# Opening stages of a hybrid encoder layer: loads in a fixed order, the first token blocks beside the memory's products, and stores on GpSimd's queue

## The chip, the core and the metric

One core of one Trainium2 chip runs the whole kernel. The metric is the device time of one execution in microseconds (us), given as the median of three runs. The profile shows one more execution of the same program. Its engines are TensorE (PE, with its weight loads PEld), VectorE (DVE), ScalarE (ACT), GpSimd (POOL) and SyncE (SP). SP computes nothing here: it issues transfers. GpSimd computes and issues transfers too.

## The reference

The kernel computes one encoder layer with three branches that read one combined projection:

```python
h = rms_norm(x, norm_pre_w)                       # x: 2048 tokens x 1024
proj = h @ w_in                                   # 1024 x 5648 columns
aq, ak, av, bqkv, ba, bb, mq, z = split(proj)
y_a = axial_gqa_attention(rope(rms_norm(aq)), rope(rms_norm(ak)), av)     # 8 heads, 2 of k and v
y_b = rms_norm(bidir_gated_deltanet(silu(conv(bqkv)), ba, bb))            # 4 heads, both directions
mkv = rms_norm(mem, mem_norm_w) @ w_mem_kv        # 256 memory tokens: 512 columns of keys, 512 of values
y_m = memory_cross_attention(mq, mk, mv)          # 4 heads
mix = concat(y_a, y_b, y_m) * silu(z)
out = x + rms_norm(mix @ w_out, norm_post_w)
```

The change touches only the opening: the memory keys and values, the norm of x, and the projection to `av`, `ba` and `bb`.

## The kernel before

Products are made in pairs of a high and a low part: each operand is split in two (`hi` is a cast, `lo` the remainder), and three products (hi hi, hi lo, lo hi) are added in PSUM. ScalarE makes the casts, VectorE most remainders.

**Who sets the order.** The program is traced in the order of its text, and a planner then orders each engine's instructions by simulated times, so an instruction can be issued earlier than its place in the text. A transfer made with `dma` (line 63, on SP) or `wdma` (line 74, on GpSimd) may be moved so. `late_dma` (line 68) issues on SP and is pinned: it can't go ahead of the instruction that was traced on SP just before it. Every engine works through its own list in order, and a transfer that waits for its data or its buffer holds those behind it.

**The memory (lines 305 to 378).** Two blocks of 128 memory tokens are loaded, normed, turned by TensorE (`turned`, PSUM tiles `tp_m`) and split (`mT`). `w_mem_kv` comes in four groups of 256 columns, each in two halves of 512 KB. `mem_load` (line 323) loads a half into `mraw` (two buffers) and splits it into `whi` and `wlo`; `mem_group` (line 341) makes 48 matmuls and brings the result out (`mkt` for keys, `mvt` for values). The loop at line 366 loads group g + 1 ahead of product g. In it also stand the load of the value weights (`load_group` at g = 2, the 272 columns of `av`, `ba`, `bb`; tiles `wraw` and `wparts`) and of the norm's weights (`wpre`, `wcol`).

**The tokens (lines 380 to 453).** There are 16 blocks of 128 tokens, in five rounds over q. `tok_norm(q)` (line 392) loads four blocks (tile `x`, nine buffers shared with the two memory blocks; `late_dma`), takes their squares on ScalarE, and their roots and scaling on VectorE. `tok_turn(q, kc)` (line 407) turns four pieces of 128 x 128 in one PSUM tile (tag `tp`, four buffers) and splits them into `hT` with the norm's weights. `av_proj(tb)` (line 414) makes 24 matmuls into a PSUM tile (tag `mm`, four buffers), brings the result out as `ab` and `vt` (two buffers), takes a maximum and stores `vt` to DRAM. Rounds q = 0 to 3 turn blocks 4q to 4q + 3, rounds 1 to 4 project those of the round before. Round 1 also scales and stores the memory's keys and values (`mem_keys`, `mem_values`; tiles `mk16` and `mv16` in the tag `wn`, one buffer that `wmem` and `wpre` have used before). Rounds 1 and 2 load and scale the key and query norm weights (`qk_weights`, three small transfers each). Round 3 loads the weights of the first query and key group (`wraw` through GpSimd; GpSimd also does one multiply and one subtraction for them).

Behind this stage come the key and query projections, the DeltaNet branch, attention and the output product. They aren't changed.

Of the kernel before, what the change touches and what calls it, by code (L numbers as in the profile page):

```python
# [11 lines left out]
F32 = mybir.dt.float32  # L12
# [11 lines left out]
D = 1024  # L24
# [4 lines left out]
KC = D // 128  # L29
# [8 lines left out]
def hybrid_layer(ctx: ExitStack, tc: tile.TileContext, t: dict, out, dbg=None):  # L38
# [24 lines left out]
    def dma(to, of):  # L63
        if to.dtype == F32R:
            to, of = to.bitcast(F32), of.bitcast(F32)
        Q.dma_start(to, of)

    def late_dma(to, of):

        Q.pinned = True  # L70
        dma(to, of)
        Q.pinned = False

    def wdma(to, of):
        if to.dtype == F32R:
            to, of = to.bitcast(F32), of.bitcast(F32)
        nc.gpsimd.dma_start(to, of)  # L77
# [3 lines left out]
    const2 = p0.enter_context(tc.tile_pool(name="const2", bufs=1, side="right"))  # L81
# [7 lines left out]
    v_d = scratch("v", [TB, 128, 256])  # L89
    v16_d = scratch("v16", [128, 2, TB, 256], F16)  # L90
    mqT_d = scratch("mqT", [4, 128, 2, S], F16)
    mkT_d = scratch("mkT", [128, 2, 4, NMEM], F16)
    mv16_d = scratch("mv16", [128, 2, 2, 512], F16)
# [30 lines left out]
    vs, mvs, hs_, mks, qns, kns = (scales[:, i:i + 1] for i in range(6))  # L124
# [118 lines left out]
    def norm_scale(w, s, cs, n=0, least=2.0 ** -90, to=None):  # L243

        m = const2.tile([128, 1], F32, tag="nsm", name="nsm", bufs=2)
        e = const2.tile([128, 1], I32, tag="nse", name="nse", bufs=2)
        V.tensor_reduce(m, w, axis=AX.X, op=ALU.max, apply_absolute_value=True)
        V.tensor_scalar(m, m, least, None, op0=ALU.max)
        V.tensor_scalar(e, m.bitcast(I32), 0x7f800000, None, op0=ALU.bitwise_and)
        V.tensor_scalar(s.bitcast(I32), e, -1.0, float((263 + n) << 23), op0=ALU.mult, op1=ALU.add)  # L250
        V.tensor_scalar(cs.bitcast(I32), e, 1.0, -float((9 + n) << 23), op0=ALU.mult, op1=ALU.add)
        to = w if to is None else to
        V.tensor_scalar(to, to, s, None, op0=ALU.mult)
# [23 lines left out]
    def load_group(*args, **kw):  # L277
        _, loaded = begin_group(*args, **kw)
        return loaded
# [12 lines left out]
    with tc.tile_pool(name="s0", bufs=1) as p:  # L292
# [13 lines left out]
        wpre = p.tile([128, D], F32, tag="wn", name="wpre")  # L306
# [16 lines left out]
        def mem_load(g):  # L323
            wg = []
            for half in range(2):
                raw = p.tile([128, 4, 256], F32, tag="mraw", name="mraw", bufs=2)
                dma(raw, t["w_mem_kv"][0, 512 * half:512 * half + 512, g * 256:g * 256 + 256].rearrange("(k p) c -> p k c", p=128))
                pool, tag = (p, "mhl") if g % 2 else (wp, "whl")
                hi, lo = (pool.tile([128, 4, 256], F32R, tag=tag, name=n, bufs=4) for n in ("whi", "wlo"))
                A.copy(hi, raw)  # L330
                V.tensor_tensor(lo, raw, hi.bitcast(F32), op=ALU.subtract)
                wg.append((hi, lo))
            return wg

        wg = mem_load(0)
# [5 lines left out]
        def mem_group(g, wg):  # L341
            ps = mm_ps(f"mem{g}", (128, 2, 256))
            for u in range(2):
                sl = slice(u * 128, u * 128 + 128)
                n = 0
                for kc in range(KC):
                    hi, lo = wg[kc // 4]
                    k = kc % 4
                    for i, (m_, w_) in enumerate(((0, hi), (1, hi), (0, lo))):
                        st, sp = (n == 0), (n == 3 * KC - 1)  # L350
                        if g < 2:
                            T.matmul(ps[:, u, :], w_[:, k, sl], mT[m_][:, kc, :], start=st, stop=sp)
                        else:
                            T.matmul(ps[:, u, :], mT[m_][:, kc, sl], w_[:, k, :], start=st, stop=sp)
                        n += 1
            if g >= 2:
                mv = mvt[:, :, (g - 2) * 256:(g - 1) * 256]
                A.copy(mv, ps)
                V.tensor_reduce(mvmax[:, g - 2:g - 1], mv, axis=AX.XY, op=ALU.max, apply_absolute_value=True)
                return  # L360
            mk = mkt[:, 2 * g:2 * g + 2]
            A.copy(mk, ps)
            V.tensor_reduce(mkmax[:, g:g + 1], mk, axis=AX.XY, op=ALU.max, apply_absolute_value=True)

        mkt = p.tile([128, 4, NMEM], F32, tag="mkt", name="mkt")
        for g in range(4):
            nxt = mem_load(g + 1) if g < 3 else None
            if g == 2:
                wav, (avcs,) = load_group([(1280, 256), (3072, 16)], dma)
            if g == 1:  # L370
                late_dma(wpre, t["norm_pre_w"].to_broadcast([128, D]))
                wcol = const2.tile([128, KC], F32, name="wcol")
                late_dma(wcol, t["norm_pre_w"].rearrange("o (k p) -> p (o k)", p=128))
                norm_scale(wpre, hs_, hcs, to=wcol)
            mem_group(g, wg)
            wg = nxt
        hT.extend(hpool.tile([128, 2, KC, 512], F16, tag="B16", name=f"hT{b}", bufs=6, align_bytes=512).rearrange("p i k c -> i p k c") for b in range(4))
        hs = {}

        def qk_weights(which):  # L380

            nw = t["k_norm_w"] if which == 0 else t["q_norm_w"]
            wb = const2.tile([128, 2, 128], F32, name=f"wb{which}")
            dma(wb[:, 0, :], nw.to_broadcast([128, 128]))
            nv = nw.rearrange("o (a s d) -> o a s d", a=2, s=2)
            wv = wb[:, 1, :].rearrange("p (a s d) -> p a s d", a=2, s=2)
            for s_ in range(2):
                dma(wv[:, :, s_, :], nv[:, :, 1 - s_, :].to_broadcast([128, 2, 32]))
            norm_scale(wb.rearrange("p a d -> p (a d)"), *((kns, kncs) if which == 0 else (qns, qncs)), n=1, least=2.0 ** -45)
            return wb  # L390

        def tok_norm(q):

            ss = p.tile([128, 4], F32, tag="ss", name=f"ss{q}", bufs=2)
            rst = p.tile([128, 4], F32, tag="rst", name=f"rst{q}", bufs=2)
            hs[q] = []
            for j in range(4):
                tb = 4 * q + j
                xt = p.tile([128, D], F32, tag="x", name=f"x{tb}", bufs=9)
                late_dma(xt, t["x"][0, tb * 128:(tb + 1) * 128, :])  # L400
                row_stats(xt, ss[:, j:j + 1], hT[q][0][:, 2 * j:2 * j + 2, :])
                hs[q].append(xt)
            rsqrt(p, rst, ss, [128, 4], 1.0 / D, EPS)
            for j in range(4):
                V.tensor_scalar(hs[q][j], hs[q][j], rst[:, j:j + 1], None, op0=ALU.mult)
# [8 lines left out]
        def av_proj(tb):  # L414
            ps = mm_ps(f"av{tb}")
            tok_proj(ps[:, 0:272], wav, tb)
            A.activation(ab[:, tb, :], ps[:, 256:272], AF.Copy, scale=avcs)
            vt = p.tile([128, 256], F32, tag="vt", name=f"vt{tb}", bufs=2)
            A.activation(vt, ps[:, 0:256], AF.Copy, scale=avcs)
            V.tensor_reduce(vmax[:, tb:tb + 1], vt, axis=AX.X, op=ALU.max, apply_absolute_value=True)  # L420
            dma(v_d[tb], vt)

        def mem_values():
            pow2_scale(mvmax, mvs, mvcs, "mv")
            mv16 = p.tile([128, 2, 2, 512], F16, tag="wn", name="mv16")
            A.activation(mv16[:, 0], mvt, AF.Copy, scale=mvs)
            V.scalar_tensor_tensor(mv16[:, 1], mvt, mvs, mv16[:, 0], op0=ALU.mult, op1=ALU.subtract)
            dma(mv16_d, mv16)

        def mem_keys():  # L430
            pow2_scale(mkmax, mks, mkcs, "mk")
            mk16 = p.tile([128, 2, 4, NMEM], F16, tag="wn", name="mk16")
            split_evac(mkt, mk16[:, 0], mk16[:, 1], mks)
            dma(mkT_d, mk16)

        wbs = []
        tok_norm(0)
        for q in range(5):
            if q in (1, 2):
                wbs.append(qk_weights(q - 1))  # L440
# [3 lines left out]
            if q == 3:  # L444
                nxt = load_group([(1024, 256)])
# [11 lines left out]
    with tc.tile_pool(name="s1", bufs=1) as p:  # L457
# [49 lines left out]
        for which in range(2):  # L507
            wb = wbs[which]
# [19 lines left out]
            for g in range(1 if which == 0 else 4):  # L528
                wg, (qcs,) = nxt
                for b in range(4):  # L530
                    if g == 0 and b < 3:
                        tables(b + 1)
                    if b == 1:
                        nxt = load_group([((which + g) * 256 if which + g < 4 else 1536, 256)])
# [49 lines left out]
    with tc.tile_pool(name="s2", bufs=1) as p:  # L584
        wg, bcs, xbs, svs, kts_ = {0: nxt[0]}, {0: nxt[1]}, {}, {}, {}
# [248 lines left out]
    with tc.tile_pool(name="s3g", bufs=1, side="right") as p:  # L834
# [4 lines left out]
        xa, ax, u, s_, s2, acc = (tmp(n) for n in ("xa", "ax", "u", "s_", "s2", "acc"))  # L839
# [69 lines left out]
    with tc.tile_pool(name="s3a", bufs=1) as sv0:  # L909
        p = rows  # L910
# [24 lines left out]
        for hp in range(2):  # L935
            p = (sv0, sv1)[hp]
# [3 lines left out]
            for d in range(2):  # L940
                for b in range(4):
                    o = 64 * d + 16 * b
# [13 lines left out]
            for d, ft in enumerate(((rr, ni), (ni, rr))):  # L956
                for n in range(2):
                    for b in range(4):
                        o = 64 * d + 16 * b
# [648 lines left out]
```

## Time and profile before

| what | value |
|---|---|
| runs | median 2408.82 us (2407.42 to 2410.19, three runs) |
| profiled execution, its own time | 2418.02 us |
| its span | 2416.0 us |
| TensorE busy | 2316.7 us (96%) |
| VectorE, ScalarE, GpSimd busy | 1637.6, 1298.9, 703.2 us |
| first product of the memory | 18.79 us |
| last value product ends, first key and query product starts | 116.06 us |

A row of the order of time gives the start and the length in us, the engine, the line, the operation, what it writes and reads by the program's names, its shape and count, and in brackets how long the engine had been idle before it and what ended that. Nearly all rows name line 51, through which every engine's instructions are issued, so tile names tell them apart: `m`, `tp_m`, `mT` and `mem` are the memory's, `x`, `tp` and `hT` the tokens', `av` and `vt` the value product's. In a row by stretches each engine's busy time stands in front of its count of instructions.

### The profile page before, as it was taken

The numbers are of one execution on the slowest core, as the hardware profiler recorded it, in microseconds if no ns is written. First come the engines' busy times: TensorE is split into PE (matmuls) and PEld (weight loads), VectorE is DVE, ScalarE is ACT, GpSimd is POOL, SyncE is SP. The second block draws the span as 40 slices with busy tenths as digits, with TensorE's granted clock in tenths as the row PEclk, the third lists the DMA queues.
The fourth block names the chain that finished last, engine by engine and source line by source line (L and its number), as shares of the span: only waits on it lengthen the run. The fifth ranks groups of instructions, "written<-read, shape, count | busy, mean of one in ns | idle before, by whom it ended". The sixth has DMA issues, their size and how long they took to land. (4 is left out here: it accounts for less than half of the span.)

```text
span 2416.0 us, 42155 instructions
## 1 busy us (share of the span) xinstructions
PE 2316.7 (96%) x15838; PEld 1466.6 (61%) x15846; DVE 1637.6 (68%) x3304; ACT 1298.9 (54%) x2508; POOL 703.2 (29%) x432
## 2 busy tenths in 40 slices
PE   6999999999999899999999999999999999899998
PEld 6888864455554347667664566666666666544443
DVE  6687658999758745555553778777888877355553
ACT  5634436544443145555543888888888788111110
POOL 0155431112211221121020554444444445122120
PEclk9999999999999999999999999999999999999999
DMA  6457656334487466677865999999999999775551
GB/s 232 144 137 162 123 118 188 101 111 126 146 254 214 106 201 212 205 221 219 249 201 192 232 248 242 246 240 244 239 250 241 246 240 231 202 248 187 178 183 53
DMA packets 949500, 471.58 MB, mean 195 GB/s; under 512 B 723184, under 2 KB 898864, under 8 KB 949040
## 3 DMA queue, kind: packets, MB, share of 16 engines
q1 hardware_dynamic: 936848, 425.89, 69.6%
q0 software_dynamic: 12448, 43.00, 5.3%
q8 instruction: 125, 2.05, 0.3%
q14 instruction: 79, 0.65, 0.1%
HBM read 207.60 MB, written 108.10 MB: 131 GB/s over the span
## 5 line engine op out<-in xcount | busy, mean ns | idle before, releaser
L51 PEld LDWEIGHTS <-wparts 128*128 128x128 f16 x3072 | 294.9, 99 | 324.2 <-issue 18.1
L51 POOL TENSOR_TENSOR hla<-Pa,hla 128x1281 f16<-128x1281 f32 x128 | 335.8, 2624 | 343.1 <-DVE hla L51 320.2
L51 DVE TENSOR_REDUCE mxa<-sa 128x1 f32<-128x1024 f32 x256 | 313.1, 1223 | 132.3 <-PE sa L51 132.2
L51 PE MATMUL sa<-K,qa 128*128 128x512 f16 x1536 | 373.8, 379 | 21.2 <-ACT Pa L51 10.0
L51 PE MATMUL z<-hT,wparts 128*128 128x512 f16 x1536 | 378.4, 384 | 4.1 <-POOL wparts L51 2.9
L51 PE MATMUL pva<-PT,V 128*128 128x256 f16 x3072 | 376.4, 273 | 0.0
L51 ACT ACTIVATE Pa<-sa,mxa,misc 128x1024 f32<-128x1024 f32 x256 | 305.9, 1199 | 97.8 <-POOL hla L51 81.0
L51 PEld LDWEIGHTS <-V 128*128 128x128 f16 x3072 | 300.6, 98 | 84.9
L51 PE MATMUL o<-wo,mhl 128*128 128x512 f16 x1416 | 309.5, 382 | 6.3 <-ACT mhl L51 3.8
L51 PE MATMUL b<-hT,wparts 128*128 128x512 f16 x1152 | 258.1, 381 | 0.0
L51 PEld LDWEIGHTS <-mhl 128*128 128x128 f16 x1464 | 143.7, 98 | 181.9 <-DVE mhl L51 4.2
L51 PEld LDWEIGHTS <-qa 128*128 128x128 f16 x1536 | 150.1, 98 | 157.0 <-issue 27.0
L51 ACT CAST hla<-Pa 128x2048 f16<-128x2048 f32 x128 | 243.0, 1899 | 4.2
L51 PEld LDWEIGHTS <-hT 128*128 128x128 f16 x2304 | 224.8, 98 | 30.4 <-DVE we L51 1.7
L51 PE MATMUL q<-wparts,hT 128*128 128x256 f16 x1920 | 210.3, 273 | 1.4 <-DVE we L51 1.4
L77 POOL DMA_DIRECT2D gate<-zg x64 | 35.4, 554 | 423.7 <-DVE zg L51 288.1
L51 POOL TENSOR_SCALAR wraw<-wraw,wsc 128x1024 f32<-128x1024 f32 x21 | 69.1, 3292 | 288.4 <-DVE wy L51 197.5
L51 ACT CAST mhl<-mr 128x2048 f16<-128x2048 f32 (+1 forms) x16 | 29.1, 1818 | 221.7 <-PE o L51 172.8
L51 DVE SCALAR_TENSOR_TENSOR y<-xb,convw,y 128x512 f32<-128x512 f32 x192 | 145.8, 771 | 2.0
L51 POOL TENSOR_TENSOR mg<-mg 128x1536 f32<-128x1536 f32 (+1 forms) x16 | 59.4, 3712 | 234.1 <-DMA mg<-r 171.2
L51 DVE SCALAR_TENSOR_TENSOR hla<-Pa,hla 128x768 f16<-128x768 f32 x128 | 121.6, 950 | 0.0
L51 DVE TENSOR_TENSOR mhl<-mr,mhl 128x2048 f16<-128x2048 f32 (+1 forms) x16 | 45.2, 2824 | 89.3 <-ACT mhl L51 89.3
(354 smaller groups left out, 3165.4 us busy)
## 6 DMA issues: line engine op xcount, KB each, us to landing
xx<-bx SPq DMA_DIRECT2D x64, 512.0 KB, 6.0
wraw<-in_w_in POOLq DMA_DIRECT2D x42, 512.0 KB, 5.3
wor<-in_w_out SPq DMA_DIRECT2D x32, 512.0 KB, 4.3
gate<-zg POOLq DMA_DIRECT2D x64, 256.0 KB, 4.0
NI<-nit SPq DMA_DIRECT2D x32, 512.0 KB, 3.0
mr<-mix SPq DMA_DIRECT2D x13, 1024.0 KB, 6.1
mg<-r SPq DMA_DIRECT2D x13, 768.0 KB
x<-in_x SPq DMA_DIRECT2D x16, 512.0 KB, 6.3
```

Source lines behind the costliest of these rows:

```text
L51: ins = f(*args, **kw)
L77: nc.gpsimd.dma_start(to, of)
```

## The change

- The loop over the memory groups moves down in the text, behind the functions that it now calls. `tok_norm(0)`, the loads and norm of the first four token blocks, stands behind the first memory product instead of behind the last.
- The load and split of the value weights stand behind the second product instead of ahead of the third.
- The loads of `w_mem_kv`, of the value weights and of the key and query norm weights are pinned (`late_dma`). With the token blocks they form one fixed order on SP: the weights of groups 0 and 1, blocks 0 to 3, group 2, `wpre` and `wcol`, the value weights, group 3, blocks 4 to 7, key norm weights, blocks 8 to 11, query norm weights, blocks 12 to 15.
- The 16 stores of `vt` and those of `mk16` and `mv16` are issued by GpSimd (`wdma`) instead of SP.

```diff
@@ mem_load
-                dma(raw, t["w_mem_kv"][0, 512 * half:512 * half + 512, g * 256:g * 256 + 256].rearrange("(k p) c -> p k c", p=128))
+                late_dma(raw, t["w_mem_kv"][0, 512 * half:512 * half + 512, g * 256:g * 256 + 256].rearrange("(k p) c -> p k c", p=128))
@@
         mkt = p.tile([128, 4, NMEM], F32, tag="mkt", name="mkt")
-        for g in range(4):
-            nxt = mem_load(g + 1) if g < 3 else None
-            if g == 2:
-                wav, (avcs,) = load_group([(1280, 256), (3072, 16)], dma)
-            if g == 1:
-                late_dma(wpre, t["norm_pre_w"].to_broadcast([128, D]))
-                wcol = const2.tile([128, KC], F32, name="wcol")
-                late_dma(wcol, t["norm_pre_w"].rearrange("o (k p) -> p (o k)", p=128))
-                norm_scale(wpre, hs_, hcs, to=wcol)
-            mem_group(g, wg)
-            wg = nxt
@@ qk_weights
-            dma(wb[:, 0, :], nw.to_broadcast([128, 128]))
+            late_dma(wb[:, 0, :], nw.to_broadcast([128, 128]))
...
-                dma(wv[:, :, s_, :], nv[:, :, 1 - s_, :].to_broadcast([128, 2, 32]))
+                late_dma(wv[:, :, s_, :], nv[:, :, 1 - s_, :].to_broadcast([128, 2, 32]))
@@ av_proj
-            dma(v_d[tb], vt)
+            wdma(v_d[tb], vt)
@@ mem_values
-            dma(mv16_d, mv16)
+            wdma(mv16_d, mv16)
@@ mem_keys
-            dma(mkT_d, mk16)
+            wdma(mkT_d, mk16)
@@
         wbs = []
-        tok_norm(0)
+        for g in range(4):
+            nxt = mem_load(g + 1) if g < 3 else None
+            if g == 1:
+                late_dma(wpre, t["norm_pre_w"].to_broadcast([128, D]))
+                wcol = const2.tile([128, KC], F32, name="wcol")
+                late_dma(wcol, t["norm_pre_w"].rearrange("o (k p) -> p (o k)", p=128))
+                norm_scale(wpre, hs_, hcs, to=wcol)
+            mem_group(g, wg)
+            if g == 0:
+                tok_norm(0)
+            if g == 1:
+                wav, (avcs,) = load_group([(1280, 256), (3072, 16)], late_dma)
+            wg = nxt
         for q in range(5):
```

## Prediction

> **What bounds the kernel now.** I read the page first, for the engine that is the bound, then the view by stretches, cut where TensorE's rows change character, then the order of time of each engine in the first 120 us.
>
> ```profile
> PE 2316.7 (96%) x15838; PEld 1466.6 (61%) x15846; DVE 1637.6 (68%) x3304; ACT 1298.9 (54%) x2508; POOL 703.2 (29%) x432
> ...
> 0.00:18.80 18.80, 3.92 (x17) 3.15 (x17) 10.03 (x28) 8.48 (x13) 0.68 (x6) 1.00 0.77 243
> 27.40:51.40 24.00, 20.72 (x166) 19.39 (x165) 20.21 (x58) 14.10 (x22) 1.72 (x2) 1.00 0.62 209
> 51.40:79.70 28.30, 28.29 (x244) 24.17 (x242) 18.49 (x45) 16.24 (x33) 1.50 (x2) 1.00 0.50 181
> 79.70:84.40 4.70, 0.02 (x1) 0.05 (x1) 2.72 (x13) 4.42 (x10) 0.00 (x0) 0.76 1.01 384
> 84.40:89.50 5.10, 4.96 (x25) 4.24 (x26) 4.47 (x13) 4.48 (x10) 0.00 (x0) 0.55 0.27 89
> 89.50:116.00 26.50, 26.50 (x235) 23.26 (x234) 18.56 (x40) 17.55 (x37) 6.55 (x4) 1.00 0.24 76
> 180.00:300.00 120.00, 118.94 (x1092) 106.61 (x1093) 83.26 (x139) 53.75 (x69) 58.81 (x61) 1.00 0.67 141
> ```
>
> The columns after a stretch's length are TensorE, its weight loads, VectorE, ScalarE, GpSimd, then the granted TensorE clock, the DMA share and GB/s. TensorE is the bound of the whole (96%), and it is full from 89.5 us on and in the query stage. So what the first stage ends earlier the kernel ends earlier, as long as nothing behind it hangs on something else. The first stage is where TensorE isn't full: it has 3.92 us of work in the first 18.8, loses 3.28 us (24.00 less 20.72) from 27.4 to 51.4, and stands still for 4.7 us from 79.7 on, after which its clock is 0.55. I read on there.
>
> ```profile
> 12.49 1.97 PE L51 MATMUL tp_m<-ident,m 128*128 128x128 f32 x8 [1.24 <-DVE m L51]
> 18.79 1.31 PE L51 MATMUL mem<-mT,whi 128*128 128x256 f32 x2 [4.33 <-ACT mT L51]
> ...
> 17.06 1.11 ACT L51 ACTIVATE wparts<-wraw 128x1088 bf16<-128x1088 f32 x1 [4.25 <-DMA wraw<-in_w_in]
> ...
> 18.17 0.56 ACT L51 CAST mT<-tp_m 128x512 fp32r<-128x512 f32 x1
> ...
> 12.35 2.35 DVE L51 TENSOR_TENSOR wlo<-mraw,whi 128x1024 fp32r<-128x1024 f32 x2
> 14.62 1.28 DVE L51 TENSOR_TENSOR mT<-tp_m,mT 128x512 fp32r<-128x512 f32 x2
> ```
>
> The memory's transposes end at 14.46 (12.49 + 1.97). ScalarE, which brings them out of PSUM (mT), had the square of the value weights (wraw) ahead of them in its order and stood 4.25 us for that transfer; TensorE's first memory product waits for the cast behind it.
>
> ```profile
> 13.87 2.95 SPq L51 DMA_DIRECT2D x<-in_x  x4
> 16.93 0.38 SPq L51 DMA_DIRECT2D mraw<-in_w_mem_kv  x1
> 17.36 1.38 SPq L51 DMA_DIRECT2D x<-in_x  x2
> 18.84 0.58 SPq L51 DMA_DIRECT2D mraw<-in_w_mem_kv  x1
> 20.22 1.67 SPq L51 DMA_DIRECT2D x<-in_x  x2
> ...
> 38.45 2.88 SPq L51 DMA_DIRECT2D mraw<-in_w_mem_kv  x2
> ...
> 70.63 0.32 SPq L51 DMA_DIRECT2D mv<-mv  x1
> 71.04 4.42 SPq L51 DMA_DIRECT2D x<-in_x  x8
> ...
> 84.38 3.65 PE L51 MATMUL tp<-ident,x 128*128 128x128 f32 x16 [4.68 <-DVE x L51]
> 88.17 1.47 PE L51 MATMUL av<-wparts,hT 128*128 128x272 f16 x8
> 89.48 0.60 PE L51 MATMUL tp<-ident,x 128*128 128x128 f32 x4
> ```
>
> These are SP's queue and, in the last three rows, TensorE after its stop. Token blocks 8 to 15 are issued at 71.04, all together, right behind the store of the memory values, which had to wait for its data. The last weights had been sent by 41.3 (38.45 + 2.88), and block 8's buffer, that of the second memory block, had been free since about 14.5. TensorE runs dry at 79.7 and waits 4.68 us for VectorE's scaled x.
>
> **The change part by part.** (1) The value weights' loads go behind the second memory product, so their squares can't stand ahead of mT. ScalarE's last two casts, 0.56 each, can follow 14.46; VectorE is busy until 15.90 (14.62 + 1.28) with the first two remainders, then makes the others, 0.64 each. The first product needs casts alone (about 15), the second a remainder (16.6), so I take 16.0 against 18.79: 2.8 us. Bounds: 0, if another wait takes the place, and the 4.25 of the row.
>
> (2) The weights of the memory groups no longer share the queue with blocks 4 to 7. Group 1's are issued as VectorE frees the two staging buffers (the middle and the end of its wlo row, 13.5 and 14.7, instead of 16.93 and 18.84); the eight blocks of 13.87 to 21.9 become four, and the others come behind group 3. Of the 3.28 us that TensorE lost from 27.4 to 51.4 I take 1.5. Bounds 0 and 3.28; not all, since VectorE worked 20.21 of those 24.00 us, on work that stays and is now wanted sooner.
>
> (3) The stores of memory keys, memory values and v leave SP, so blocks 8 to 11 stand behind loads alone. Late next is a buffer: blocks 9 to 11 take those of blocks 0 to 2, free when the first four blocks are turned. What follows an issue, and what covers it:
>
> ```profile
> DMA to landing us min/median/max: 6.0/6.3/10.7
> ...
> L51 ACT ACTIVATE hT<-x x16: 1040/1057/1076, 20.2 to 85.0; 128x1024 bf16<-128x1024 f32 x16
> ...
> 81.30 0.17 DVE L51 TENSOR_SCALAR rs_x<-ss 128x4 f32<-128x4 f32 x1 [2.85 <-ACT hT L51]
> ...
> 83.48 0.76 DVE L51 TENSOR_SCALAR x<-x,rst 128x1024 f32<-128x1024 f32 x1
> ...
> 105.31 0.60 PE L51 MATMUL tp<-ident,x 128*128 128x128 f32 x4
> 105.75 10.47 PE L51 MATMUL av<-wparts,hT 128*128 128x272 f16 x89
> 116.06 1.15 PE L51 MATMUL q<-wparts,hT 128*128 128x256 f16 x9
> ```
>
> 6.3 to land, 4 x 1.06 of squares, 2.2 of the root (81.30 to 83.48), 0.76 of scaling: 13.5 us from the release to the first turn. TensorE's cover is four value products, 96 matmuls at 0.116 (105.75 to 116.06 over 89), 11.1 us, and 32 turns at 0.11 (105.31 to 105.75 over four), 3.5 us: 14.6. So the stop of 4.68 closes, with a margin of 1.1 us only. I take 4.7 and charge new waits in (5). Bounds 0 and 4.7.
>
> (4) Without the stop the clock doesn't fall. Behind it 16 turns took 3.79 us (84.38 to 88.17) where 16 x 0.11 is 1.76, and eight value matmuls 1.31 (88.17 to 89.48) where 8 x 0.116 is 0.93: 2.4 us, all or nothing with (3). [...]
>
> (5) The six loads of the key and query norm weights leave the queue's first 8 us and stand behind blocks 4 to 7 and 8 to 11. That gains nothing: the memory blocks stood ahead of them. VectorE, which works in order, may now stand for them:
>
> ```profile
> DMA to landing us min/median/max: 7.7/7.7/7.7
> ...
> L77 POOL DMA_DIRECT2D gate<-zg x24: 540/544/588, 633.2 to 893.9; - x24
> ...
> DMA to landing us min/median/max: 2.6/4.0/8.0
> ...
> L51 ACT ACTIVATE vt<-av,wc x16: 455/467/553, 59.4 to 116.4; 128x256 f32<-128x256 f32 x16
> ...
> DMA to landing us min/median/max: 1.7/1.7/3.4
> ...
> 97.91 2.85 POOL L51 TENSOR_SCALAR wraw<-wraw,wsc 128x1024 f32<-128x1024 f32 x1 [44.95 <-issue]
> 103.37 2.14 POOL L51 TENSOR_TENSOR wparts<-wraw,wparts 128x1024 f16<-128x1024 f32 x1 [2.61 <-ACT wparts L51]
> ```
>
> The first row is their landing (7.7 us), so VectorE can lose 0 to 7.7 us, most of it behind value products. With the thin margin of (3) I charge 1.4 us for new waits of both kinds, near the lower end, because these loads can be issued long before the stage that they belong to.
>
> (6) The 18 stores go to GpSimd: 18 x 0.54 (the gate's store, twice as large as v's) is 9.8 us on an engine that stood idle 44.95 us before 97.91. Behind a store that waits for its value product there stand the first query group's multiply (2.85) and subtraction (2.14). These ended at 105.51, 10.6 us ahead of the first query product at 116.06: cover for the wait of three value products. Cost nothing; without cover 5.0.
>
> Sum: 2.8 + 1.5 + 4.7 + 2.4 - 1.4 = 10.0 us less. The profiled execution took 2418.02 by its own time, 9.2 above the median of the runs; the terms are differences inside its span, so I take them off the median: 2408.8 - 10.0 = 2398.8. The query stage only starts earlier. Behind it the planner may order things otherwise; I allow 2 us either way, twice what TensorE lost from 180 to 300.
>
> **The rivals.** *The stop comes back.* Blocks 9 to 11 wait for the turns of blocks 0 to 3, which now compete with the memory products' work on VectorE. If they, or the norm weights, are 5.8 us later than I think, the margin of 1.1 and the gap's 4.7 are used up and the slow clock is back: 10.0 - 4.7 - 2.4 = 2.9 less, 2405.9. For it speaks the margin; against it, that VectorE idled 9.8 us from 51.4 to 79.7 (28.30 less 18.49).
>
> *The stores on GpSimd's queue hold the values.* vt has two buffers. A v store lands 1.7 us after its issue now; on GpSimd's queue the gate's took 4.0, at most 8.0. A value product takes 24 x 0.116, 2.8 us, so two buffers give 5.6 us for a cast (0.47), an issue (0.54) and the landing. At 4.0 that fits. At 8.0 each product is 1.7 late, 27 us over 16, of which four PSUM buffers take 11: 16 less the gain of 10 is 6 slower, 2415. It decides from a landing of 7.2 on, where loss and gain are equal. [...]
>
> *More than that:* every gain at its upper bound and no new wait, 4.25 + 3.28 + 4.7 + 2.4 = 14.6, 2394.2.
>
> *No effect:* another early square stands ahead of mT and x is still late; then (2)'s 1.5 is left, 2407.3.
>
> **How the numbers follow.** About 0.2%, 4.8 us, can be told from no change here. Forecast 0.57 (2395 to 2403), more than that 0.10, the stop back 0.14, no effect 0.07, stores holding the values 0.06, and 0.06 for an order of the later stages that costs more than the gain. Faster: the first two and half of the stop's return, 0.74. Same: the other half and no effect, 0.14. Slower: 0.12. The range from 2391 (the better case with the later stages some 3 us in its favour) to 2411 leaves out some 0.15.
>
> **What would show it.** Right: the first memory product near 16 us; on SP no x behind a store; no gap of TensorE over 2 us between 20 and 105; a granted clock of 1.00 in every stretch behind 30; the first query product near 106 instead of 116. (1) is wrong if ScalarE again waits for a transfer ahead of mT; (2) if the memory products end later than 45; (3) if a turn waits over 3 us for VectorE's x; (5) if VectorE waits for a norm weight; (6) if GpSimd's subtraction of the first group ends after the first query product. The whole is wrong if the first query product comes 10 us earlier and the end doesn't.

## The result and the profile after

The changed kernel took 2394.74 us (median of six runs, 2392.97 to 2397.48) beside 2407.66 us for the kernel before (six runs, 2406.07 to 2410.19): a ratio of 0.9948, with a 95% interval of 0.9936 to 0.996. That is 12.9 us less, where 10.0 were forecast. Two more comparisons on other chips, told below, gave 5.0 and 5.3 us less (0.9981 [0.9967, 0.9994] and 0.9979 [0.9966, 0.9991]). So the kernel is faster, by 0.2 to 0.5%. The profiled execution took 2394.83 us by its own time, its span was 2393.1 us. Three executions in the whole record, among them the profiled one of after_third, took 2988 to 2994 us at a granted clock of 0.753; they are left out of every time here, and after_third's profile isn't used.

By stretches (length; then TensorE, weight loads, VectorE, ScalarE, GpSimd; granted clock, DMA share, GB/s), the changed kernel:

```profile
0.00:18.80 18.80, 6.37 (x26) 5.49 (x27) 11.76 (x30) 8.96 (x12) 0.69 (x6) 1.00 0.57 185
...
27.40:51.40 24.00, 22.23 (x179) 21.40 (x178) 20.85 (x56) 18.88 (x31) 0.00 (x0) 0.93 0.69 227
51.40:79.70 28.30, 23.14 (x186) 19.29 (x184) 21.56 (x64) 20.99 (x42) 6.45 (x10) 0.94 0.69 239
79.70:100.00 20.30, 20.17 (x175) 17.03 (x173) 18.98 (x41) 15.41 (x31) 11.18 (x11) 1.00 0.29 100
```

TensorE has 2.45 us more work done in the first 18.8 us (6.37 against 3.92). The stop at 79.7 is gone. But the stretch from 51.4 to 79.7, which was full before (28.29 of 28.30), now has 23.14, and the clock there is 0.94, not 1.00; from 27.4 to 51.4 it is 0.93. The stop has moved forward. In the order of time:

```profile
14.46 0.58 PE L51 MATMUL mem<-mT,whi 128*128 128x256 f32 x1
16.74 0.58 PE L51 MATMUL mem<-mT,whi 128*128 128x256 f32 x1 [1.70 <-DVE mT L51]
...
36.95 0.66 PE L51 MATMUL mem<-whi,mT 128*128 128x256 f32 x2 [1.77 <-ACT whi L51]
...
37.49 2.80 PE L51 MATMUL tp<-ident,x 128*128 128x128 f32 x12
...
46.06 0.28 PE L51 MATMUL mem<-wlo,mT 128*128 128x256 f32 x1
...
47.48 1.78 PE L51 MATMUL av<-wparts,hT 128*128 128x272 f16 x14
...
63.35 0.27 PE L51 MATMUL p2mv<-ident,p2mmv 128*1 128x128 f32 x1 [3.74 <-DVE rs_u L51]
63.46 1.82 PE L51 MATMUL tp<-ident,x 128*128 128x128 f32 x12
...
65.73 2.00 PE L51 MATMUL av<-wparts,hT 128*128 128x272 f16 x8
69.06 1.16 PE L51 MATMUL tp<-ident,x 128*128 128x128 f32 x6 [1.33 <-DVE p2mmv L51]
...
111.72 0.49 PE L51 MATMUL q<-wparts,hT 128*128 128x256 f16 x3
...
35.85 1.04 ACT L51 CAST whi<-mraw 128x1024 fp32r<-128x1024 f32 x1 [0.22 <-DMA mraw<-in_w_mem_kv]
...
44.38 0.42 DVE L51 TENSOR_REDUCE nsm<-wb 128x1 f32<-128x256 f32 x1 [1.68 <-DMA wb<-in_k_norm_w]
...
53.09 2.74 DVE L51 TENSOR_SCALAR x<-x,rst 128x1024 f32<-128x1024 f32 x4
...
60.55 0.42 DVE L51 TENSOR_REDUCE nsm<-wb 128x1 f32<-128x256 f32 x1 [2.55 <-DMA wb<-in_q_norm_w]
...
63.06 0.14 DVE L51 TENSOR_REDUCE p2mmv<-mvmax 128x1 f32<-128x2 f32 x1
...
65.87 2.74 DVE L51 TENSOR_SCALAR x<-x,rst 128x1024 f32<-128x1024 f32 x4
...
68.85 0.15 DVE L51 COPY p2mmv<-p2mv 128x1 f32<-128x1 f32 x1
...
30.63 1.52 SPq L51 DMA_DIRECT2D mraw<-in_w_mem_kv  x2
...
37.30 15.02 SPq L51 DMA_DIRECT2D x<-in_x  x4
52.37 1.67 SPq L51 DMA_DIRECT2D wb<-in_q_norm_w  x3
...
54.15 20.87 SPq L51 DMA_DIRECT2D x<-in_x  x4
...
92.30 2.68 POOL L51 TENSOR_TENSOR wparts<-wraw,wparts 128x1024 f16<-128x1024 f32 x1 [0.52 <-ACT wparts L51]
```

Read the second stop backwards. TensorE stands 3.74 us until 63.35, and what it then issues is no turn: it is p2mv, the small product that spreads the maximum of the memory's values. The turns right behind it (63.46) had their scaled x at 55.83 (53.09 + 2.74). They were ready, and TensorE's order put the product ahead of them. That product needs p2mmv, which VectorE writes at 63.06. VectorE came to it late because it stood 2.55 us until 60.55 for the query norm weights, then scaled them and took a root; they had been issued at 52.37, behind blocks 8 to 11, with which SP stood 15.02 us until buffers came free. So three things that have nothing to do with one another stand in one line: a buffer, a norm weight, a memory scale. Whether the norm weight is the price or only the last in the line, an experiment has to say.

The 1.33 us that TensorE stands until 69.06 hang on the same scale. What it issues there are still turns of blocks 4 to 7: a round has 32 turns, and 12 ran at 63.46, 8 run at 69.06 (the view of that row ends at 70.00 and counts six), 4 at 71.66 and 8 of the 12 at 72.91. The spread maximum takes one of the four PSUM buffers of the turns (`pow2_scale` and `tok_turn` share the tag `tp`), so the fourth tile of this round has p2mv's buffer, and it is free when VectorE's copy at 68.85 has read it. That copy stands behind the scaling of blocks 8 to 11 (65.87 + 2.74 = 68.61). The first turn of blocks 8 to 11 comes at 73.78; the last row of SP's queue agrees, where blocks 13 to 15 get the buffers of blocks 4 to 6 just ahead of 75.02 (54.15 + 20.87).

The last value product ends and the first query product starts at 111.72, 4.3 us ahead of 116.06.

### The profile page after: what moved, and what is told of

Its sections match the earlier page's. It is cut to its first block, busy times and chain, and to the rows that moved or that the text cites. A ratio compares the mean times of both kernels' runs of the same rounds, so it can differ in the third digit from the quotient of the medians.

```text
span 2393.1 us, 42170 instructions
## 1 busy us (share of the span) xinstructions
PE 2306.3 (96%) x15846; PEld 1462.9 (61%) x15846; DVE 1640.4 (69%) x3304; ACT 1299.7 (54%) x2508; POOL 712.5 (30%) x450
```

## The experiments

All kernels' first stages in one table. "Ratio" is to the kernel before in the same comparison, with its 95% interval. The times are those at which the first row of a tile starts in the profile: the memory's first product, the first value product, the first query product, and then (rest) the length from there to the end of the last product.

| kernel | ratio | memory | values | query | rest |
|---|---|---|---|---|---|
| before (first profile) | | 18.8 | 51.4 | 116.1 | 2291.6 |
| before_again | 1.0006 [0.9993, 1.0019] | 18.7 | 51.7 | 115.3 | 2281.1 |
| order_only | 0.9998 [0.9987, 1.0008] | 14.3 | 46.2 | 115.5 | 2277.2 |
| order_second | 0.9997 [0.9984, 1.001] | 15.0 | 46.7 | 115.9 | 2277.0 |
| vt_only | 1.0001 [0.999, 1.0012] | 18.4 | 50.6 | 118.6 | 2276.8 |
| two_stores | 0.9974 [0.9961, 0.9988] | 18.4 | 53.3 | 112.3 | 2275.9 |
| stores_only | 0.9958 [0.9942, 0.9973] | 18.6 | 52.3 | 110.8 | 2272.0 |
| stores_second | 0.9969 [0.9956, 0.9981] | 18.6 | 55.3 | 113.9 | 2274.0 |
| after | 0.9948 [0.9936, 0.996] | 14.5 | 47.5 | 111.7 | 2272.9 |
| after_again | 0.9981 [0.9967, 0.9994] | 14.4 | 45.9 | 110.2 | 2275.6 |
| after_third | 0.9979 [0.9966, 0.9991] | | | | |
| norm_weights_free | 0.9966 [0.9952, 0.9981] | 14.4 | 45.9 | 109.5 | 2275.2 |
| late_av | 0.9978 [0.9964, 0.9991] | 14.5 | 52.5 | 115.2 | 2268.8 |
| scales_late | 0.9954 [0.9938, 0.997] | 14.5 | 49.5 | 111.5 | 2272.3 |

Four kernels ran together on a chip each time: before_again, stores_only, order_only and norm_weights_free (kernel before: 2402.14 us); two_stores, late_av, scales_late and after_again (2402.16); vt_only, stores_second, order_second and after_third (2403.13). The theory at the start was that of the prediction, with the later stages as its rival, since the first stages' 4.3 us aren't 12.9.

Each label has one profile, and the starts in it scatter: stores_only and stores_second are one kernel, and their first query products stand 3.1 us apart, because the memory's products end at 52.4 in one and at 55.4 in the other. The length from the first value product to the first query product repeats better: 58.5 and 58.7 us in these two, 64.2 and 64.3 in after and after_again, 69.3 and 69.2 in the two of the order, 64.6 and 63.5 in the kernel before. So readings below that go by this length are firmer than those that go by a start.

**The two halves.** The change has a part in the stores and a part in the order of loads.

before_again, nothing changed:

> The kernel before, unchanged, profiled once more. The two profiles so far stand 22.9 us apart in their spans (2416.0 and 2393.1) while the medians differ by 12.9, and only 4.3 us of that lie ahead of the first query product (116.06 and 111.72). Theory A (the first profile of before was a slow execution in its later stages, and a usual one still loses some us there against the changed kernel): span 2404 to 2408, first query product at 116.0 to 116.2, and 2289 to 2292 us from there to the end, 8 us above the changed kernel's 2281.4. Theory B (the later stages are alike, since their instructions stand in the same order, and all 12.9 us belong to the first stage): first query product later than 116, near 124, and about 2281 from there on.

Theory A held for the later stages: the span was 2404.6 us, and 2289.4 from the first query product to its end (the column "rest" ends with the last product, some 8 us sooner). The first query product came at 115.3, a little ahead of the 116.0 that it named. So the 12.9 us don't all belong to the first stage.

stores_only and stores_second, the kernel before with `wdma` in three places:

```
-            dma(v_d[tb], vt)
+            wdma(v_d[tb], vt)
...
-            dma(mv16_d, mv16)
+            wdma(mv16_d, mv16)
...
-            dma(mkT_d, mk16)
+            wdma(mkT_d, mk16)
```

> The kernel before with only the 18 stores moved to GpSimd's queue. Theory A (the stop at 79.7 came from the token blocks that stood behind the store of the memory values on SP, and what the first stage ends earlier the kernel ends earlier): blocks 8 to 11 are issued before 60 us, no idle TensorE over 2 us between 50 and 110, first query product at 109 (116.1 less 4.7 and 2.4), time 7 us below before. Rival B (the stop comes back behind another wait on VectorE, as in the changed kernel at 59.6): first query product at 112 to 114, 2 to 4 us below before. Rival C (GpSimd's queue holds vt): later than 116, time above before.

> All 18 stores on GpSimd's queue and the order of loads of before, once more, beside the changed kernel on one chip. Theory A (the stores carry the whole gain of the change, the order of loads none): ratio as the changed kernel's within 0.0015, 0.995 to 0.998; first query product at 110 to 111. Theory B (the order of loads is worth its 4 us in the first products after all, and the first comparison hid it): ratio 0.0015 or more above the changed kernel's.

In both the stop is gone, as Theory A of stores_only said, and in the comparison with the changed kernel Theory A of stores_second held (0.9969 beside 0.9979). The first query products, 110.8 and 113.9, missed the 109 and the 110 to 111 that were expected.

order_only and order_second, the changed kernel with the same three lines turned back to `dma`:

> The changed kernel with its 18 stores back on SP (the fixed order and the moved loop stay). Theory A (the stores on SP were what held the token blocks): blocks 8 to 15 again stand behind the store of the memory values, issued near 65 to 70, a stop of TensorE of 5 to 9 us before their first turn, first query product at 113 to 117, time 3 us below before or equal to it. Rival B (the order alone carries the gain): first query product at 112 as in the changed kernel, 10 to 13 us below before.

> The changed kernel with its 18 stores on SP, once more. Theory A: ratio 0.999 to 1.001, a gap of TensorE of 5 us or more before the turns of the third round, first query product at 114.5 to 116, DeltaNet's stage at 406 to 410. Theory B: ratio 0.997 to 0.9985, half of the changed kernel's gain.

Theory A held both times.

The stores alone gave 0.9958 and 0.9969, the order alone 0.9998 and 0.9997. On the last chip the changed kernel had 0.9979 beside 0.9969 for the stores: the order adds nothing that can be measured, nor does it take anything. Its gain is real where it arises, and lost on the way: in order_second the memory starts at 15.0 and the values at 46.7 instead of 18.7 and 51.7, and the queries at 115.9 instead of 115.3. The rows of order_second in the order of time (SP's queue, then TensorE) say where it goes:

```profile
70.09 0.34 SPq L51 DMA_DIRECT2D mv<-mv  x1
70.52 4.52 SPq L51 DMA_DIRECT2D x<-in_x  x8
...
84.64 3.40 PE L51 MATMUL tp<-ident,x 128*128 128x128 f32 x16 [8.92 <-DVE x L51]
```

As before, eight token blocks leave SP at 70.5, behind the memory values' store, and as before the turns come at 84.6 (84.38 in the kernel before). TensorE merely waits 8.92 us there instead of 4.68. The arrival of these blocks sets the end of the stage, whatever is earlier ahead of it.

stores_only has the blocks without a store ahead of them, and no gap of 0.3 us between its first value product and its first query product. The next row is its SP queue:

```profile
55.06 20.87 SPq L51 DMA_DIRECT2D x<-in_x  x7
```

From its first value product to its first query product it takes 58.5 us, the changed kernel 64.2 us. So it starts its values 4.8 us later than the changed kernel (52.28 against 47.48) and its queries 0.9 earlier (110.8 against 111.7). With the second profiles the queries have no order (110.8 and 113.9 against 111.7 and 110.2), the two lengths keep theirs.

**Which stores.** two_stores moves only the two memory stores, vt_only only the sixteen of vt:

```
-            dma(mv16_d, mv16)
+            wdma(mv16_d, mv16)
...
-            dma(mkT_d, mk16)
+            wdma(mkT_d, mk16)
```

> The kernel before with two stores alone on GpSimd's queue: mk16 and mv16; the 16 of vt stay on SP. Theory A (the stop at 79.7 of before was SP standing at the two memory stores, with the x of later rounds behind them; the 16 stores of vt held only the cos and sin loads, 63.6 us into the first query stage): the stop is gone as in stores_only, the first query product starts near 110.5 instead of 115.3, but the stage from there to the b product stays at 211.4 instead of 210.2; about 2396 on a chip where the kernel before takes 2402, ratio 0.9975, so some 3 us short of stores_only (0.9958). Theory B (a store of vt on SP also holds an x of the next round, since each stands between two loads): a stop of 1 us or more before a turn stays between 60 and 110, the first query product at 112 to 115, ratio 0.9985 to 1.0. Theory C (the part of the gain that came behind the first query stage belongs to the vt stores): the stage from the first b product to the first z product at 283 to 284 as with all stores on SP; with two stores doing as much as eighteen it is 280.6 to 281.

```
-            dma(v_d[tb], vt)
+            wdma(v_d[tb], vt)
```

> The kernel before with the 16 stores of vt alone on GpSimd's queue; mk16 and mv16 stay on SP: the other half of two_stores. Theory A (the stop is the two memory stores; the vt stores are worth something in the later stages): a gap of 3 to 9 us before a turn between 60 and 105, first query product at 113.5 to 115.5; the stage from DeltaNet's first value product to the first score product at 402 to 405 as in the six profiles with the vt stores on GpSimd (402.2 to 405.2), against 406.8 to 412.5 in the four with them on SP; ratio 0.998 to 0.999. Theory B (that parting of six and four is chance, and the first stages alone make the difference): DeltaNet's stage anywhere from 402 to 410, ratio 0.999 to 1.0005.

SP's queue in two_stores:

```profile
56.04 1.97 SPq L51 DMA_DIRECT2D x<-in_x  x4
64.43 8.82 SPq L51 DMA_DIRECT2D v<-vt  x4
76.51 1.28 SPq L51 DMA_DIRECT2D x<-in_x  x3
```

and in vt_only, with TensorE's stop:

```profile
69.74 0.34 SPq L51 DMA_DIRECT2D mv<-mv  x1
70.13 4.67 SPq L51 DMA_DIRECT2D x<-in_x  x8
...
83.68 3.65 PE L51 MATMUL tp<-ident,x 128*128 128x128 f32 x16 [4.88 <-DVE x L51]
```

Two of the eighteen stores carry the stop (which of the two wasn't run; the blocks leave right behind that of the values): without them blocks come from 56.04 on, no gap of 0.3 us is left between the first value product and the first query product, and the ratio is 0.9974. Sixteen others without these two are worth nothing that can be measured (1.0001), and the stop stays. Theory A of the two expectations holds for the stop, but its times for the first query product were missed: 112.3 instead of 110.5 in two_stores, and 118.6 instead of 113.5 to 115.5 in vt_only, where a second gap of 1.87 us follows the stop. For the later stages it falls: vt_only's DeltaNet stage took 407.2 us, not 402 to 405, and two_stores' stage from the first b product to the first z product 281.3, as with all eighteen.

**What is left of the stop.** norm_weights_free is the changed kernel with the norm weights' six loads unpinned:

```
-            late_dma(wb[:, 0, :], nw.to_broadcast([128, 128]))
+            dma(wb[:, 0, :], nw.to_broadcast([128, 128]))
...
-                late_dma(wv[:, :, s_, :], nv[:, :, 1 - s_, :].to_broadcast([128, 2, 32]))
+                dma(wv[:, :, s_, :], nv[:, :, 1 - s_, :].to_broadcast([128, 2, 32]))
```

> The changed kernel with the six loads of the key and query norm weights unpinned again, so that they are issued in the first 10 us. Theory A (in the changed kernel VectorE stood 1.68 us at 42.7 and 2.55 us at 58.0 for these loads, and TensorE's stop of 3.74 us from 59.6 to 63.35 stands behind the second wait): both waits are gone, the stop is at most 1.5 us, first query product at 108 to 110, 2 to 4 us below the changed kernel. Rival B (the stop has the token blocks 8 to 11 and the memory scales behind it, whatever VectorE waits for): the stop moves or stays at 3 us or more, first query product at 111 to 112, time within 1 us of the changed kernel.

scales_late has this and calls the memory's scaling a round later:

```
-            if q == 1:
+            if q == 2:
                 mem_keys()
                 mem_values()
```

> The changed kernel with the norm weights unpinned as in norm_weights_free, and mem_keys and mem_values a round later (at q = 2), so that the broadcast products of the memory's scales (p2mk, p2mv) don't stand ahead of the turns of blocks 4 to 7 on TensorE. Theory A (after the norm weights are free, what is left of the stop is these scales, waiting for VectorE): no gap of TensorE over 1 us between the value products, the first query product at 106.5 to 108 instead of 109.5, ratio 0.995 to 0.996. Theory B (the gaps of 1.2, 0.7 and 1.5 us there come from blocks 9 to 11, whose buffers come free near 52, so that ScalarE stands for their x): gaps of the same sum wherever the scales stand, first query product at 109 to 110, ratio 0.996 to 0.997 as norm_weights_free.

ScalarE, VectorE and TensorE in norm_weights_free:

```profile
56.56 1.06 ACT L51 ACTIVATE hT<-x 128x1024 bf16<-128x1024 f32 x1 [2.90 <-DMA x<-in_x]
...
65.40 2.73 DVE L51 TENSOR_SCALAR x<-x,rst 128x1024 f32<-128x1024 f32 x4
...
47.60 4.91 PE L51 MATMUL av<-wparts,hT 128*128 128x272 f16 x41 [1.20 <-DVE wparts L51]
...
59.53 0.27 PE L51 MATMUL p2mv<-ident,p2mmv 128*1 128x128 f32 x1
...
61.77 0.38 PE L51 MATMUL p2mv<-p2mmv,ones 1*128 1x1 f32 x2 [0.66 <-DVE p2mmv L51]
62.56 0.66 PE L51 MATMUL tp<-ident,x 128*128 128x128 f32 x4 [0.42 <-DVE p2mmv L51]
...
64.75 1.09 PE L51 MATMUL av<-wparts,hT 128*128 128x272 f16 x4 [1.53 <-ACT hT L51]
...
68.94 0.63 PE L51 MATMUL tp<-ident,x 128*128 128x128 f32 x4 [0.86 <-DVE hT L51]
```

and ScalarE and TensorE in scales_late:

```profile
59.19 1.06 ACT L51 ACTIVATE hT<-x 128x1024 bf16<-128x1024 f32 x1 [3.24 <-DMA x<-in_x]
...
72.54 1.98 PE L51 MATMUL av<-wparts,hT 128*128 128x272 f16 x14 [2.35 <-DVE hT L51]
75.67 0.27 PE L51 MATMUL p2mv<-ident,p2mmv 128*1 128x128 f32 x1 [0.84 <-DVE p2mmv L51]
```

The wait of 3.74 us ahead of p2mv is gone once the norm weights are there (59.53, without idle time), so they were its cause. But they weren't its price. With its values started at 45.9, as in after_again, norm_weights_free has its first query product at 109.5 against 110.2: 0.7 us (63.6 us of value products against 64.3). Other gaps have come, of 1.20, 0.66, 0.42, 1.53 and 0.86 us, 4.7 in all where the changed kernel has 5.1 (3.74 and 1.33). The first of them waits for the value weights' remainder. Behind the other four, by the order of the rows, stands ScalarE, which waits 2.9 us for the x of a late block (3.2 in scales_late) with the next squares, which VectorE's root needs, and the evictions of turned blocks queued behind it; so VectorE comes to scale blocks 8 to 11 hardly sooner (65.40) than in the changed kernel (65.87). Theory A's numbers were met (no gap over 1.53 us, 109.5, and 2394.6 us beside 2397.15 on another chip), but its reading, that the two waits were the price, is not what the length of this stage shows. The times leave more open than the 0.7: the ratio is 0.9966 where the changed kernel had 0.9981 and 0.9979 (and 0.9948), each on another chip.

Moving the scales changes the places of the gaps (0.47, 2.35 and 0.84 instead of those five), their sum to 3.7. Theory B of scales_late is the better one for this stage, though its first query product, 111.5, fits neither theory: its values start 3.6 us later than those of norm_weights_free (49.5), and the length from there is 62.0 us instead of 63.6. Its ratio is the lowest of its chip all the same, 0.9954 beside 0.9981 for the changed kernel (2392.13 against 2397.15 us), with its query products 1.3 us later than after_again's (111.5 against 110.2). That difference arises in the later stages, so I don't count it as this edit's. That more buffers for x would take ScalarE's wait away wasn't tried.

**One part of the order.** late_av is stores_only with the value weights moved as in the change, and the first four token blocks left where they were:

```
-            if g == 2:
-                wav, (avcs,) = load_group([(1280, 256), (3072, 16)], dma)
...
             mem_group(g, wg)
+            if g == 1:
+                wav, (avcs,) = load_group([(1280, 256), (3072, 16)], late_dma)
```

> stores_only with the value weights' load and split behind the second memory product, as in the changed kernel; norm weights and the memory's weights unpinned, the first four token blocks at their place of before. So the changed kernel without blocks 0 to 3 beside the products and without the pinned norm weights. Theory A (the value weights' squares held the memory's first product by 3.5 to 4 us, and this gain is lost again in the changed kernel only to the waits for the norm weights and the memory's scale): first memory product near 14.5 instead of 18.0, first query product at 106.5 to 108 instead of 110.2, ratio 0.994 to 0.9950, some 3 us below stores_only. Theory B (what sets the end of this stage is the arrival of the token blocks, so that an earlier start only makes a stop longer): first memory product near 14.5 all the same, a stop of 2 to 4 us before a turn, first query product at 109.5 to 111, ratio 0.9955 to 0.9960 as stores_only.

Its rows (SP, TensorE):

```profile
30.14 1.56 SPq L51 DMA_DIRECT2D mraw<-in_w_mem_kv  x2
31.76 46.83 SPq L51 DMA_DIRECT2D x<-in_x  x16
...
48.54 3.79 PE L51 MATMUL tp<-ident,x 128*128 128x128 f32 x16 [3.04 <-DVE x L51]
```

Both theories fall. The memory's first product is at 14.5 as both had it, but the value products start at 52.5 and the queries at 115.2. I had overlooked that the token blocks now come behind all weights (31.76): the first turn waits 3.04 us for them. The two moves of the order belong together: the later value weights give the memory its early start, and in the changed kernel, where blocks 0 to 3 come beside the products, the values start at 47.5.

**The size.**

> The changed kernel once more, beside the others on one chip. All theories: ratio 0.995 to 0.9965, first query product at 111 to 112. They differ on the stages behind it. Theory A (the later gain belongs to the kernel with its stores on GpSimd): from the first query product to the end 2272 to 2274 again, from the first b product to the first z product 280.5 to 281.5. Theory B (the later stages scatter from one execution to the next, and the 2272.9 of the first profile was a draw): anything from 2272 to 2281 to the end, the b stage as likely 283 to 284.

> The changed kernel a third time, since its first two comparisons gave 0.9948 and 0.9981 with intervals that do not meet. Theory A (a chip's own level moves the ratio, since the kernels differ in where their half-clock periods fall): anything from 0.9945 to 0.9985 here, with the first stages as before, first query product at 110 to 112. Theory B (the first was a draw): 0.997 to 0.9985.

Medians were 2397.15 and 2397.81 us, 5.0 and 5.3 below the kernel before. after_again missed what all its theories shared (0.9981 instead of 0.995 to 0.9965, first query product at 110.2 instead of 111 to 112), and its 2275.6 us behind that fit Theory B alone; the ratio of after_third fits both of its theories. The 5 us are about what the first query product moved, 115.3 in before_again to 110.2 in after_again, but with a scatter of 3 us in such starts that can be chance. In the first comparison there were 12.9, of which the first profiles show 4.3 in the first stages. Most of the difference between the comparisons lies with the kernel before, 2407.66 us there and 2402.1 to 2403.1 on the other chips.

The column "rest" of the table is what the later stages took. From 40 us into the first query stage on every engine's instructions stand in the same order in the kernels before and after, and still the lengths differ: 2276.8 to 2291.6 us in the five profiles with the memory stores on SP, 2268.8 to 2275.9 in the eight with them on GpSimd. These don't overlap, yet no single stage parts them: from the first b to the first z product 280.4 to 283.7 against 279.6 to 283.6 us, the DeltaNet stage 406.8 to 412.5 against 402.2 to 407.4. One kernel alone, before, took 2291.6 and 2281.1. Whether two early stores do something to later stages, or thirteen profiles are too few, stays open.

## Why the prediction came out as it did

The time was right: 2398.8 forecast, 2394.74 measured, inside the range. The sum behind it was not, so the hit is in part luck. Its terms say 10.0 us by the first query product; that moved 4.3 us in the first profile. The rest of the first comparison's 12.9 came from stages for which the prediction allowed 2 us either way, and in two other comparisons it didn't come.

- (1), value weights' squares no longer ahead of mT: right. The first memory products came at 14.46 and 16.74, where about 15 and 16.6 were reckoned, against 18.79.
- (2), memory weights sooner: TensorE's loss from 27.4 to 51.4 fell from 3.28 to 1.77 us (24.00 less 22.23), by the 1.5 that was taken. But half-clock time has come there (a granted clock of 0.50 from 37.1 to 40.5): 24.00 us at 0.93 are some 1.7 us lost. By the prediction's own sign it is wrong in the first profile (the memory products end at 46.3, not by 45) and right in after_again (44.8). The 1.77 us stand ahead of 36.95 for a split weight of the last group: ScalarE could cast it when it had landed, at 35.85, and SP had issued it at 30.63, behind the value weights. Together (1) and (2) were to bring 4.3; the first value product came 4.0 earlier (51.44 to 47.48).
- (3), (4) and (5), the stop closes, the clock stays, and 1.4 for new waits: 4.7 + 2.4 - 1.4 = 5.7 forecast for the value products; they took 64.6 us before (51.44 to 116.06) and 64.2 after (47.48 to 111.72), a gain of 0.4. The step that failed is the charge in (5): it put new waits at 1.4 us, and there were two gaps of 3.74 and 1.33, 5.1 together, and some 1.7 us of half clock (28.30 us at 0.94).

  (3) itself came true: the memory values' store did hold the blocks, as two_stores and vt_only show, on the order of before its removal closes the stop (stores_only has none), and in the changed kernel no turn waits for VectorE's x: blocks 8 to 11 were scaled by 68.61, and their first turn is at 73.78. So the margin of 1.1 us wasn't what gave way.

  What the sum lacked is a path: the product p2mv of the memory's scale stands ahead of the turns of blocks 4 to 7 in TensorE's order and in their PSUM buffers, so what VectorE loses in front of it (2.55 us for a norm weight, of the 0 to 7.7 allowed) reaches TensorE, where (5) put most of it behind value products. By (5)'s own sign, a wait for a norm weight, it is wrong too: there were two, of 1.68 and 2.55. They alone were worth 0.7 by the length in norm_weights_free, since other waits took their place; these hang on blocks 9 to 11, whose buffers come free when blocks 0 to 3 are turned, as (3) said. The half clock that (4) was to be rid of came back with the gaps (0.50 was granted from 64.4 to 67.9, and the eight value products at 65.73 took 2.00 us, against the 0.93 of eight at 1.00).
- (6), stores on GpSimd cost nothing: right. The subtraction for the first query group ends at 94.98 (92.30 + 2.68), 16.7 us ahead of the query product. In the grouped rows of the changed kernel the sixteen stores land after 2.3 us in the median and nobody waits for them:

```profile
L77 POOL DMA_DIRECT2D v<-vt x16: 542/548/717, 57.9 to 112.9; - x16
...
DMA to landing us min/median/max: 2.0/2.3/5.6
```

Of the rivals, "The stop comes back" happened in part: gaps and half clock are back, through a norm weight and, with that away, through the late blocks, both of which it named; the memory's scale, in which they meet TensorE, it didn't name. Its price was 5.3 (5.7 less 0.4) instead of 7.1. By its reckoning the time would have been 2405.9, 2.9 below the kernel before; 5.0 and 5.3 below were measured twice.

## What to carry to other kernels

A store that waits for a late result should not stand in the queue that feeds the next stage's loads: moving two such stores out of eighteen carried this change (0.9974), and sixteen harmless ones added little (1.0001 by themselves). An earlier start ahead of a stage whose end is set by an arrival or by a buffer only lengthened the wait here: with the stores on SP the earlier first products were worth nothing (0.9998 and 0.9997; TensorE waited 8.92 us instead of 4.68). A margin counted for one chain (scaled x to the turns) covers that chain alone; a small product of another kind that stands ahead in the same engine's order needs a reckoning of its own. The row that names a wait's last link (a norm weight, 3.74 us) isn't its price; taking the link away shortened the stage by 0.7.

## What the runs showed of the hardware

In these profiles a TensorE gap doesn't lead to the half clock (a granted clock of 0.50) by its length alone. Before attention's first score product the rows of stores_only:

```profile
1288.64 2.48 PE L51 MATMUL sa<-K,qa 128*128 128x512 f16 x6 [2.31 <-DVE zg L51]
1290.91 2.16 PE L51 MATMUL z<-hT,wparts 128*128 128x512 f16 x6
1292.91 1.46 PE L51 MATMUL sa<-K,qa 128*128 128x512 f16 x6
```

and of order_only:

```profile
1300.33 1.46 PE L51 MATMUL sa<-K,qa 128*128 128x512 f16 x6 [3.09 <-DVE zg L51]
1301.62 1.46 PE L51 MATMUL z<-hT,wparts 128*128 128x512 f16 x6
1302.92 1.46 PE L51 MATMUL sa<-K,qa 128*128 128x512 f16 x6
```

The same twelve products run slow behind 2.31 us of idleness (4.27 us from 1288.64 to the third row) and at full speed behind 3.09 (2.59 to the next six score products at 1302.92). In the first profile of the kernel before they took 4.27 us behind 2.73 (1313.78 to 1318.05), with a granted clock of 0.50 from 1314.4 to 1317.8; in the changed kernel they took 2.58 behind 1.83 (1292.82 to 1295.40), at 1.00. The loss is 1.7 us: from the first score product to the 769th there pass 388.1 us in the former (1313.78 to 1701.86) and 386.4 in the latter (1292.82 to 1679.25). Shorter gaps part so too, within one profile: in the changed kernel, where 1.83 us left the score products at full speed, 12 turns took 2.46 us behind the 1.77 us ahead of 36.95 (37.49 to 39.95), at the 0.50 granted from 37.1 to 40.5. What decides it beside the length was not shown. So in this kernel a stop of some 2 to 3 us is priced with and without 1.7 us more, and two profiles of one kernel differ by such steps: from 27.4 to 51.4 the granted clock was 0.93 in after and 1.00 in after_again.
